# RMS norm and matmul on one core: another order of rows in the eight-tile transfers

## The chip, the cores and the metric

The kernel runs on one core of a Trainium2 chip. The metric is the device time in microseconds. A profile of one execution comes beside it, whose span is a little shorter than the time. The engines of a core are TensorE (PE; its weight loads are PEld), VectorE (DVE), ScalarE (ACT), GpSimd (POOL) and SyncE (SP), which here only issues transfers. Sixteen DMA engines carry these transfers between DRAM and SBUF, the on-chip memory of 128 partitions.

## What is computed

Each row of x is divided by its root mean square, scaled by gamma and multiplied by a weight matrix:

```python
def reference(x, gamma, weight, eps):          # x: 16 x 1024 x 512 float32
    rms = np.sqrt(np.mean(x ** 2, axis=-1, keepdims=True) + eps)
    x_norm = x / rms * gamma                   # gamma: 512
    return np.matmul(x_norm, weight).astype(np.float32)   # weight: 512 x 768
```

There are 16 x 1024 = 16,384 rows. 33.6 MB of x come in, 50.3 MB of results go out, and rows are independent of each other, so that it doesn't matter which row lies in which partition as long as its result goes back to the same row.

## The kernel before

The rows are cut into 128 tiles of 128 rows, one row in each partition. A tile is cast to bf16 (`cast`, L93), transposed by TensorE (`transpose_word`, L120), copied out of PSUM by VectorE (`evac`, L127) and multiplied with the weights in four steps of 128 (`matmul`, L155). Gamma has been folded into the weights at the start. Meanwhile ScalarE squares and sums the rows (`square`, L97), and takes the root (`root`, L101); VectorE takes the reciprocal (L103). The result of a tile is scaled by it on its way from PSUM to the output tile: even tiles by ScalarE (L137), odd tiles by VectorE (L139). Casts are GpSimd's, but for the opening. Most of this goes in pairs of tiles: a loop over 64 pairs from L266 issues, for each pair, the cast of a pair three ahead, the squares of the next, and the matmuls of this one with transposes of a pair two ahead between them. The order within each engine is written out by hand (`tc.manual_schedule`), so the program's order is the order of issue.

Rows come and go in groups of G = 8 tiles, NG = 16 groups in all. A group has one input tile `xt` of 128 partitions x 8 x 512 float32 (five such buffers, L65) and one output tile `ot` of 128 x 8 x 768 float32 (three, L72). Which row of DRAM lies in which partition is set by one function, `rows` (L59). For the first group (i < G) it serves small pieces, of one and two tiles. For the others partition p holds the eight consecutive rows 8p to 8p + 7 of the group's 1,024, one for each of its eight tiles. In DRAM these are one stretch of 8 x 512 x 4 bytes = 16 KB of x, or 8 x 768 x 4 bytes = 24 KB of out, and the partitions follow each other without a gap.

All large transfers are issued by SyncE, in one queue. `load` (L82) brings a group, or a part of it where `stretches` says so (group 1 comes as two halves of four tiles). `store` (L152) sends a group once its last tile is scaled; group 14 goes as two halves, and group 15 as pieces of 2, 2, 2, 1 and 1 tiles. `load_until(2 * j + AHEAD)` with AHEAD = 28 (L267) issues a load some 28 tiles ahead of the pair that TensorE works on. As both kinds stand in one queue, a load issued behind a store goes out after the store's own wait for the outputs.

Of the kernel before, what the change touches and what calls it, by code (L numbers as in the profile page):

```python
# [18 lines left out]
def kernel(  # L19
# [9 lines left out]
    P = 128  # L29
# [8 lines left out]
    G = 8  # L38
# [4 lines left out]

    def stretches(parts):
        first, size, i = {}, {}, 0
        for g in range(NG):
            for n in parts.get(g, [G]):
                for t in range(i, i + n):  # L50
                    first[t], size[t] = i, n
                i += n
        return first, size

    opening = [1, 2, 1, 2, 2]
    x_first, x_size = stretches({0: opening, 1: [4, 4]})
    o_first, o_size = stretches({0: opening, NG - 2: [4, 4], NG - 1: [2, 2, 2, 1, 1]})

    def rows(ap, i, n):  # L59
        if i < G:  # L60
            return ap[i * P:(i + n) * P, :].rearrange("(p t) d -> p t d", t=n)
        return ap.rearrange("(g p t) d -> g p t d", p=P, t=G)[i // G, :, i % G:i % G + n, :]

    singles = ctx.enter_context(tc.tile_pool(name="singles", bufs=1))
    xin = ctx.enter_context(tc.tile_pool(name="xin", bufs=5))  # L65
# [13 lines left out]
    def load(i):  # L79
        if i // G not in x_tiles:  # L80
            x_tiles[i // G] = xin.tile([P, G, D], F32, name="xt")
        nc.sync.dma_start(out=held(x_tiles, i, x_size[i]), in_=rows(x, i, x_size[i]))  # L82
# [58 lines left out]
    def accumulator():  # L141
        return opsum.tile([P, 2, WIDE], F32, name="ops").rearrange("p a b -> p (a b)")
# [6 lines left out]
    def store(i):  # L149
        first, n = o_first[i], o_size[i]  # L150
        if i == first + n - 1:
            nc.sync.dma_start(out=rows(out, first, n), in_=held(o_tiles, first, n))  # L152
# [32 lines left out]
    with tc.manual_schedule():  # L185
# [80 lines left out]
        for j in range(2, NP):  # L266
# [15 lines left out]
            for i, engine in ((2 * j, nc.scalar), (2 * j + 1, nc.vector)):  # L282
                a = accumulator()
# [4 lines left out]
        for i in (NT - 2, NT - 1):  # L288
            for lo, hi, engine in ((0, WIDE, nc.scalar), (WIDE, O, nc.vector)):
                a = accumulator()  # L290
# [39 lines left out]
```

## Time and profile before

| What | Value |
|---|---|
| time, median of 3 runs | 211.11 us (210.84 to 211.83) |
| span of the profiled execution | 209.0 us |
| TensorE busy | 198.7 us (95%) |
| ScalarE busy | 158.3 us (76%) |
| VectorE busy | 111.6 us (53%) |
| GpSimd busy | 66.4 us (32%) |
| DRAM read, written | 35.13 MB, 50.33 MB |
| mean rate of the DMA engines | 410 GB/s |
| stores of eight tiles, 13 | 3,072 KB each, 20.5 us from issue to landing (median) |
| loads of eight tiles, 14 | 2,048 KB each, 24.9 us from issue to landing (median) |

The shares are of the span and overlap, since the engines work side by side. Landing is when the transfer's last byte is reported; the time from issue to landing holds the wait behind transfers issued earlier. In the lines that follow, a name such as `xb L93` is a tile and the line of the program that made it, and `A <- B` in a table of waits says that A stood idle until B was done.

### The profile page before, as it was taken

The numbers are of one execution on the slowest core, as the hardware profiler recorded it, in microseconds if no ns is written. First come the engines' busy times: TensorE is split into PE (matmuls) and PEld (weight loads), VectorE is DVE, ScalarE is ACT, GpSimd is POOL, SyncE is SP. The second block draws the span as 40 slices with busy tenths as digits, with TensorE's granted clock in tenths as the row PEclk, the third lists the DMA queues.
The fourth block names the chain that finished last, engine by engine and source line by source line (L and its number), as shares of the span: only waits on it lengthen the run. The fifth ranks groups of instructions, "written<-read, shape, count | busy, mean of one in ns | idle before, by whom it ended". The sixth has DMA issues, their size and how long they took to land.

```text
span 209.0 us, 3555 instructions
## 1 busy us (share of the span) xinstructions
PE 198.7 (95%) x1268; PEld 137.5 (66%) x1293; DVE 111.6 (53%) x204; ACT 158.3 (76%) x388; POOL 66.4 (32%) x71
## 2 busy tenths in 40 slices
PE   7899999999999999999999999999999999999960
PEld 3466776667666776677666766676666766776630
DVE  2566565466456545644654565466456545645630
ACT  4599678778877877887787778778777877887830
POOL 1165443233323323332332333233223323310000
PEclk9999999999999999999999999999999999999997
DMA  6999999999999999999999999999999999998983
GB/s 223 413 426 444 396 404 422 423 448 411 433 426 417 455 415 442 408 439 415 423 448 415 445 408 448 430 415 444 408 444 423 434 437 426 409 423 357 412 347 142
DMA packets 7206, 85.69 MB, mean 410 GB/s; under 512 B 1042, under 2 KB 1044, under 8 KB 3220
## 3 DMA queue, kind: packets, MB, share of 16 engines
q1 hardware_dynamic: 6912, 85.46, 97.0%
q8 instruction: 10, 0.16, 0.3%
q10 hardware_dynamic: 276, 0.00, 0.1%
q14 instruction: 8, 0.07, 0.1%
HBM read 35.13 MB, written 50.33 MB: 409 GB/s over the span
## 4 chain that ended last, share of the span: by engine, by line
PE 93%; DVE 2%; issue 1%; ACT 1%
PE ops L155 78%; PE tp L120 13%; PE ops L210 1%; DVE ot L139 1%; DVE xT L127 1%; ACT ot L137 0%; ACT jk L97 0%; DVE xb L93 0%; DVE w_bf L139 0%; PE tp L224 0%; ACT rms L101 0%; DVE warm L201 0%; DVE rstd L103 0%; DVE eps_sb L203 0%
## 5 line engine op out<-in xcount | busy, mean ns | idle before, releaser
L155 PE MATMUL ops<-w_bf,xT 128*128 128x512 bf16 (+1 forms) x999 | 192.5, 324 | 1.9 <-DVE w_bf L139 0.6
L155 PEld LDWEIGHTS <-xT 128*128 128x128 bf16 x1024 | 100.2, 98 | 57.0 <-issue 1.0
L93 POOL CAST xb<-xt 128x1024 bf16<-128x1024 f32 (+1 forms) x65 | 65.7, 1016 | 118.5 <-PE tp L120 108.1
L127 DVE COPY xT<-tp 128x1024 bf16<-128x1024 bf16 (+1 forms) x67 | 44.5, 667 | 80.8 <-PE tp L120 80.8
L137 ACT ACTIVATE ot<-ops,rstd 128x768 f32<-128x768 f32 (+1 forms) x65 | 58.1, 894 | 37.7 <-PE ops L155 36.9
L97 ACT ACTIVATE jk<-xt 128x512 bf16<-128x512 f32 x128 | 78.8, 619 | 1.2 <-DMA xt<-in_x_dram 1.2
L120 PE MATMUL tp<-ident_f,xb 128*128 128x128 f32 x256 | 69.0, 274 | 0.3 <-DVE xb L93 0.2
L139 DVE TENSOR_SCALAR ot<-ops,rstd 128x768 f32<-128x768 f32 (+1 forms) x65 | 64.5, 992 | 2.9 <-PE ops L155 2.8
L120 PEld LDWEIGHTS tp<-ident_f,xb 128*128 128x128 f32 x256 | 35.9, 141 | 3.8 <-issue 0.8
L97 ACT ACTIVATION_READ_ACCUMULATOR jk<-xt 128x1 f32 x128 | 24.4, 190 | 0.0
L101 ACT ACTIVATE rms<-ssq,eps_sb 128x2 f32<-128x2 f32 (+1 forms) x64 | 18.9, 295 | 2.0
L103 DVE RECIPROCAL rstd<-rms 128x2 f32<-128x2 f32 (+1 forms) x64 | 9.9, 155 | 3.2 <-ACT rms L101 3.1
L210 PE MATMUL ops<-warm 128*128 128x512 bf16 x11 | 4.5, 555 | 1.2 <-DVE eps_sb L203 1.2
L210 PEld LDWEIGHTS <-warm 128*128 128x128 bf16 x11 | 1.4, 134 | 2.6 <-issue 1.4
L137 ACT ACTIVATE w_bf<-w_f,g_sb 128x768 bf16<-128x768 f32 x2 | 1.9, 936 | 1.4 <-DMA w_f<-in_weight_dram 0.7
L192 ACT ACT_TABLE_LOAD x1 | 1.3, 1283 | 1.8 <-issue 1.8
L93 DVE CAST xb<-xt 128x512 bf16<-128x512 f32 x2 | 1.1, 530 | 2.5 <-DMA xt<-in_x_dram 2.5
L139 DVE TENSOR_SCALAR w_bf<-w_f,g_sb 128x512 bf16<-128x512 f32 (+2 forms) x3 | 1.4, 480 | 0.5 <-DMA w_f<-in_weight_dram 0.5
L224 PEld LDWEIGHTS tp<-ident_f,g_row 2*128 2x128 f32 x2 | 0.3, 200 | 0.8 <-issue 0.8
L201 DVE MEMSET warm<- 128x256 uint32 x1 | 0.3, 272 | 0.9 <-PEq L311 0.9
L224 PE MATMUL tp<-ident_f,g_row 2*128 2x2 f32 x2 | 0.4, 264 | 0.0
masks.py:199 POOL TENSOR_SCALAR_AFFINE_SELECT ident_f<-ident_f 128x128 f32<-128x128 f32 x1 | 0.3, 294 | 0.1
(7 smaller groups left out, 0.8 us busy)
## 6 DMA issues: line engine op xcount, KB each, us to landing
out_dram<-ot SPq DMA_DIRECT2D x13, 3072.0 KB, 20.5
xt<-in_x_dram SPq DMA_DIRECT2D x14, 2048.0 KB, 24.9
out_dram<-ot SPq DMA_DIRECT2D x6, 768.0 KB, 7.0
out_dram<-ot SPq DMA_DIRECT2D x2, 1536.0 KB, 9.0
xt<-in_x_dram SPq DMA_DIRECT2D x2, 1024.0 KB, 11.1
xt<-in_x_dram SPq DMA_DIRECT2D x3, 512.0 KB, 5.7
w_f<-in_weight_dram SPq DMA_DIRECT2D x2, 768.0 KB, 6.0
out_dram<-ot SPq DMA_DIRECT2D x4, 384.0 KB, 17.9
```

Of the source, the lines that this page charges most:

```text
L93: engine.tensor_copy(out=xb_tiles[i // 2][:, i % 2:i % 2 + n, :], in_=held(x_tiles, i, n))
L97: nc.scalar.activation(out=jk, in_=held(x_tiles, i)[:, 0, :], func=AF.Square, accum_out=ssq)
L101: nc.scalar.activation(out=rms[:, :n], in_=ssq[:, :n], func=AF.Sqrt, scale=1.0 / D, bias=eps_sb)
L103: nc.vector.reciprocal(out=rstd[:, :n], in_=rms[:, :n])
L120: nc.tensor.transpose(out=tp_tiles[j][:, t, h, :], in_=words[:, lo:lo + P], identity=ident_f)
L127: nc.vector.tensor_copy(out=dst[:, t:t + n, :], in_=src[:, t:t + n, :])
L137: nc.scalar.mul(out=dst, in_=src, mul=r)
L139: nc.vector.tensor_single_scalar(out=dst, in_=src, scalar=r, op=mybir.AluOpType.mult)
L155: nc.tensor.matmul(out=acc[:, lo:hi], lhsT=xT_tiles[i // 2][:, i % 2, k // 2, :, k % 2], rhs=w_bf[:, k, lo:hi], start=(k == 0), stop=(k == ...
L192: nc.scalar.preload_act_table(AF.Sqrt)
L210: nc.tensor.matmul(out=spare[:, :WIDE], lhsT=warm[:, :P], rhs=warm, start=True, stop=True)
L224: nc.tensor.transpose(out=gp[:, c, :], in_=g_row[:, :, c], identity=ident_f[:2, :2])
```

## The change

One line in `rows` differs. A group's 1,024 rows were split as (p t), with p the partition. Now they are split as (b a t), with a = 16 and b = 8, and the partition is 8a + b. A partition still holds eight consecutive rows, so the stretches keep their length, but stretch number 16b + a in DRAM now goes to partition 8a + b, where stretch number p went to partition p. The same function serves loads and stores, so that each row's result returns to its place.

```diff
     def rows(ap, i, n):
         if i < G:
             return ap[i * P:(i + n) * P, :].rearrange("(p t) d -> p t d", t=n)
-        return ap.rearrange("(g p t) d -> g p t d", p=P, t=G)[i // G, :, i % G:i % G + n, :]
+        return ap.rearrange("(g b a t) d -> g a b t d", a=16, b=P // 16, t=G)[i // G, :, :, i % G:i % G + n, :]
```

The idea is this. If each of the 16 DMA engines carries eight neighbouring partitions, as the change assumes, then engine a carries the eight values of b for its a. Before, that was a block of eight stretches of its own, far from those of the other engines. After, the 16 engines in step work on the 16 stretches of one b, which lie side by side in DRAM, and then all move on to the next 16. On the DRAM side the pattern now has two dimensions where it had one, 16 by 8 in place of 128.

## The prediction

> **What bounds the kernel now.** I read the share of each engine and the DMA line first, then the chain of waits, the table of who waited for whom, the issues of the DMA queue in order of time, and last a table of 10 us windows. On the page:
>
> ```profile
> span 209.0 us, 3555 instructions
> ...
> PE   7899999999999999999999999999999999999960
> ...
> DMA  6999999999999999999999999999999999998983
> ...
> q1 hardware_dynamic: 6912, 85.46, 97.0%
> ...
> PE 93%; DVE 2%; issue 1%; ACT 1%
> ```
>
> Two rows are full in nearly every slice: TensorE, and the mean of the 16 DMA engines. The last line is the chain that ended last: 93% of it is TensorE, so today TensorE sets the end. But the DMA engines have nothing to spare. Queue 1 moved 85.46 MB in 97.0% of 16 engines' 209.0 us, which is 0.970 x 16 x 209.0 = 3,244 us of engine time, or 85.46 MB / 3,244 us = 26.3 GB/s for one busy engine. Who waits for whom:
>
> ```profile
> POOL xb L93 <- PE tp L120: 108.1, 53, 4.5
> DVE xT L127 <- PE tp L120: 80.8, 63, 1.4
> ACT ot L137 <- PE ops L155: 36.9, 62, 1.3
> POOL xb L93 <- DMA xt<-in_x_dram: 9.8, 4, 3.9
> ```
>
> The columns are us in total, how often, and the longest. The engines wait for TensorE. Waits of the casts for loaded rows are 9.8 us in 4 pieces, and no line says that an output tile waited for an earlier store. The rhythm is in the DMA queue's issues (start, us):
>
> ```profile
> 58.47 0.33 SPq L152 DMA_DIRECT2D out_dram<-ot  x1
> 58.90 0.88 SPq L82 DMA_DIRECT2D xt<-in_x_dram  x1
> 70.62 0.33 SPq L152 DMA_DIRECT2D out_dram<-ot  x1
> 71.04 0.81 SPq L82 DMA_DIRECT2D xt<-in_x_dram  x1
> ```
>
> One store of eight tiles and one load of eight tiles go out every 70.62 - 58.47 = 12.15 us, TensorE's time for eight tiles. They carry 3,072 + 2,048 KB = 5.243 MB, so the pace asks for 5.243 MB / 12.15 us = 431.5 GB/s. The windows say what is delivered (the last two columns are the DMA share and GB/s):
>
> ```profile
> 100.00:110.00 10.00, 9.95 (x67) 6.98 (x66) 5.95 (x11) 7.89 (x21) 3.57 (x4) 1.00 1.01 433
> ...
> 200.00:210.00 10.00, 2.07 (x14) 1.13 (x12) 1.50 (x3) 1.37 (x2) 0.00 (x0) 0.84 0.55 220
> ```
>
> Demand and supply meet to within a per cent. A store issued at 46.3 us lands after 20.2 us and one issued at 143.5 us after 21.1 us: the queue in front of the engines neither empties nor grows much. So TensorE is the bound by name and the DMA engines are a second bound just underneath; whatever makes a transfer slower comes out in the time.
>
> [...]
>
> **The change part by part.** In the built program the instructions are the same in number and order on every engine; only the shapes of the transfers differ. A store's DRAM side was 128x6144 and is 16x8x6144. This holds for every transfer of groups 1 to 15 (G = 8 and i >= G in `rows`), the four-, two- and one-tile pieces among them; the opening eight tiles and the weights keep their form.
>
> 1. What stays, at cost nothing: bytes, number of transfers, the length of a stretch (16 KB of x, 24 KB of out, since t and d are still neighbours in DRAM), partitions and TensorE's work. The queue's issue of a transfer, 0.33 to 0.96 us, may grow with one dimension more; SyncE waits 168.6 us of the span for VectorE's outputs, which hides a doubling of some 45 issues.
>
> 2. The order in DRAM. Stretch p = 8a + b moves from place p to place 16b + a. Consecutive stretches of a partition run are now 256 KB (x) or 384 KB (out) apart. [...] I put the cost at zero. The gain is bounded by what is lost now[...] and hidden under TensorE except after its end. TensorE ends at about 202 us; the last store (384 KB, issued at 202.7) lands 5.4 us later. A 256 KB load of the opening landed 2.9 us after its issue, so 384 KB with the engines free would take about 2.9 + 128 KB / 431.5 GB/s = 3.2 us. At most 2.2 us is to be had.
>
> 3. Which engine touches which partition. This is the part that decides. [...]
>
> What is stretched: 15 groups x 12.15 us = 182.3 us of the DMA engines' time. The DMA engines are full now, and buffers can't pay for a lower rate: an output buffer (three of eight tiles) is wanted again two groups, 24.3 us, after its store, which lands in 20.5 us; 3.8 us of slack, once. Behind a late landing stand the scalings of ScalarE and VectorE (L137, L139), behind them TensorE for an accumulator. Behind a late load stand GpSimd's cast and ScalarE's squares, then the transposes. So the time is 211.1 + 182.3 x (f - 1).
>
> f is not in the trace. [...] I take 1.65[...]: 211.1 + 182.3 x 0.65 = 330 us. The ends kept for the range are f = 1.1 (229 us) and f = 2.0 (393 us).
>
> **The rivals.** (a) Sharing hurts in one direction only, or softly. Loads are 15 x 2.097 = 31.5 MB, at 431.5 GB/s 73 us; doubled alone they give 284 us. Soft sharing, f from 1.05 to 1.4, gives 220 to 284. [...] (b) No change: the engines are dealt out as before[...]. TensorE's 12.15 us stays the pace: 211 us. For it: TensorE has 93% of the chain, and 26.3 GB/s may be an engine's own limit. [...] (c) Faster: neighbouring stretches save waits in DRAM and the engines end more evenly. It can take only from the 2.2 us of the drain; half of it gives 210.0 us. [...]
>
> **How the numbers follow.** Forecast, sharing in both directions with f from 1.4 to 2.0: 0.60. Rival (a): 0.25. Rival (b): 0.08. Rival (c): 0.07. Slower by over 0.5% is 0.60 + 0.25 = 0.85. The range from 228 to 394 leaves out (b) and (c), 0.15, and about 0.05 of the softest sharing and of anything worse than in step.
>
> **What would show it.** If right: the DMA row stays near full while the rate falls from 410 towards 85.69 MB / 328 us = 261 GB/s; store and load landings grow from 20.5 and 24.9 us by the same factor or more; waits for xt and for the stores of ot appear among the engines' own; TensorE's busy share falls to about 198.7 / 328 = 61% with the same number of instructions and the same means for scalings and casts. Step 2 is wrong if the rate falls although one engine's partitions stay as before, or if only the order of rows without the shape of 16 does it. Step 3 is wrong if the rate stays at 410 GB/s and the store interval at 12.15 us; the prediction then falls as a whole. If only loads are long, rival (a) holds.

## The result, and the profile after

The changed kernel takes 255.69 us (median of 6 runs, 252.79 to 256.92) where the kernel before takes 211.16 us (median of 6). That is 44.5 us more. Runs within 1.5% of the fastest count as fast, and the ratio of fast runs alone is 1.203, with a 95% interval from 1.194 to 1.212. The row of rates before the change, and then the page of the changed kernel:

```profile
GB/s 223 413 426 444 396 404 422 423 448 411 433 426 417 455 415 442 408 439 415 423 448 415 445 408 448 430 415 444 408 444 423 434 437 426 409 423 357 412 347 142
```

```profile
span 251.0 us, 3555 instructions
...
DMA  7999999999999999999999999999999999999940
GB/s 260 388 225 225 230 221 323 301 281 248 338 341 300 411 326 428 367 418 394 413 375 401 422 422 409 418 419 418 410 394 437 416 394 380 394 320 299 306 165 22
...
q1 hardware_dynamic: 6912, 85.46, 95.5%
...
DMA 53%; PE 32%; DVE 3%; ACT 2%; issue 1%; POOL 0%; ACTq 0%; SPq 0%
...
out_dram<-ot SPq DMA_DIRECT2D x13, 3072.0 KB, 29.6
xt<-in_x_dram SPq DMA_DIRECT2D x14, 2048.0 KB, 34.8
```

The DMA engines are as full as before, yet move less. The row GB/s, one number for each of 40 slices (of 6.3 us in the changed kernel), tells where. After the opening it falls to 221 to 230 for four slices, half of the 431.5 GB/s that TensorE asks for. Then it climbs, is at 394 to 437 in most slices of the middle, and drops again in the last five. The loss is thus not spread over the run. More than half of the chain is now transfers. The table of who waited for whom has lines that were not there or were small:

```profile
POOL xb L94 <- DMA xt<-in_x_dram: 50.4, 14, 8.7
ACT ot L138 <- DMA out_dram<-ot: 42.1, 10, 8.2
...
DVE ot L140 <- DMA out_dram<-ot: 18.6, 9, 5.9
PE ops L156 <- ACT ot L138: 17.0, 9, 5.6
```

GpSimd's casts wait for loaded rows (50.4 us, before 9.8), and both scaling engines wait for an output buffer whose store has not landed; behind them TensorE waits for an accumulator. The store issues give the delay group by group (start, us):

```profile
68.30 0.59 SPq L153 DMA_DIRECT2D out_dram<-ot  x1
...
88.14 0.59 SPq L153 DMA_DIRECT2D out_dram<-ot  x1
...
102.19 0.59 SPq L153 DMA_DIRECT2D out_dram<-ot  x1
...
156.81 0.59 SPq L153 DMA_DIRECT2D out_dram<-ot  x1
...
168.96 0.59 SPq L153 DMA_DIRECT2D out_dram<-ot  x1
```

The first two are 19.84 us apart; the last two are at TensorE's old 12.15 us. Before the change, the store of group 5, third in these lines, went out here:

```profile
82.76 0.33 SPq L152 DMA_DIRECT2D out_dram<-ot  x1
```

Against the same stores before, group 5 is 102.19 - 82.76 = 19.4 us late, group 11 is 181.27 - 155.64 = 25.6 us late, the last store is 232.7 - 202.7 = 30.0 us late, and the end is 42.0 us late. So 19.4 us go in the first five groups, 6.2 in the next six, 4.4 in the rest, and 12.0 after the last store's issue, which lands 17.3 us later where it took 5.4. Three questions follow. Is it the shape of 16 or the order in DRAM? Do both directions suffer? Why does the rate recover, and then fall again?

### The profile page after: what moved, and what is told of

Same layout as the page of the kernel before. It is cut to its first block, busy times and chain, and to the rows that moved or that the text cites. A ratio compares the mean times of both kernels' runs of the same rounds, so it can differ in the third digit from the quotient of the medians.

```text
span 251.0 us, 3555 instructions
## 1 busy us (share of the span) xinstructions
PE 204.3 (81%) x1268; PEld 138.8 (55%) x1293; DVE 114.9 (46%) x204; ACT 155.8 (62%) x388; POOL 66.1 (26%) x71
## 3 DMA queue, kind: packets, MB, share of 16 engines
q1 hardware_dynamic: 6912, 85.46, 95.5%
## 4 chain that ended last, share of the span: by engine, by line
DMA 53%; PE 32%; DVE 3%; ACT 2%; issue 1%; POOL 0%; ACTq 0%; SPq 0%
DMA out_dram<-ot 53%; PE ops L156 26%; PE tp L121 4%; DVE ot L140 2%; ACT ot L138 2%; PE ops L211 2%; POOL xb L94 0%; DVE xT L128 0%; ACT jk L98 0%; DVE w_bf L140 0%; PE tp L225 0%; ACT rms L102 0%; DVE warm L202 0%; ACTq L138 0%; SPq L153 0%
## 5 line engine op out<-in xcount | busy, mean ns | idle before, releaser
L156 PE MATMUL ops<-w_bf,xT 128*128 128x512 bf16 (+1 forms) x999 | 197.5, 328 | 18.9 <-ACT ot L138 17.0
L156 PEld LDWEIGHTS <-xT 128*128 128x128 bf16 x1024 | 101.3, 99 | 58.7 <-issue 3.1
L94 POOL CAST xb<-xt 128x1024 bf16<-128x1024 f32 (+1 forms) x65 | 65.4, 1015 | 147.6 <-PE tp L121 88.7
L121 PE MATMUL tp<-ident_f,xb 128*128 128x128 f32 x256 | 69.9, 277 | 6.5 <-POOL xb L94 6.4
## 6 DMA issues: line engine op xcount, KB each, us to landing
out_dram<-ot SPq DMA_DIRECT2D x13, 3072.0 KB, 29.6
xt<-in_x_dram SPq DMA_DIRECT2D x14, 2048.0 KB, 34.8
out_dram<-ot SPq DMA_DIRECT2D x2, 1536.0 KB, 20.5
```

The costliest lines, as they stand in the source:

```text
L94: engine.tensor_copy(out=xb_tiles[i // 2][:, i % 2:i % 2 + n, :], in_=held(x_tiles, i, n))
L121: nc.tensor.transpose(out=tp_tiles[j][:, t, h, :], in_=words[:, lo:lo + P], identity=ident_f)
L156: nc.tensor.matmul(out=acc[:, lo:hi], lhsT=xT_tiles[i // 2][:, i % 2, k // 2, :, k % 2], rhs=w_bf[:, k, lo:hi], start=(k == 0), stop=(k == ...
```

## The experiments

The expectations weigh two theories. By the DRAM-order theory the wider steps of a partition run in DRAM slow the transfers. "Ports theory" is their name for the sharing that the forecast assumed: with the shape 16x8 DMA engines slow each other while they are in step. f is the factor by which the transfers of groups 1 to 15 then take longer, and a lag is the distance between two engines, in us or in packets (a packet is what is moved for one partition). The traces show the slowing: between 20 and 40 us a load's packet of 16 KB takes 1.25 us in the changed kernel, where it took 0.61 before (medians). They don't show which engine carries which partitions, nor which engines slow each other and through what; the pairs of the expectations are an assumption.

### The order in DRAM without the slowest dimension of 16

```diff
-        return ap.rearrange("(g b a t) d -> g a b t d", a=16, b=P // 16, t=G)[...]
+        return ap.rearrange("(g b a t) d -> g a b t d", a=32, b=P // 32, t=G)[...]
```

> Neighbouring stretches in DRAM for the 16 engines as in the changed kernel (partition 4a + b holds stretch 32b + a), but the slowest dimension is 32[...]. Ports theory [...]: back to 211 us, within 2 us, TensorE's 12.15 us a group and over 425 GB/s in the steady part. DRAM-order theory (the wide steps in DRAM slow the reads and writes): about as slow as the changed kernel, 245 to 260 us.

211.08 us (median of 14), ratio to the kernel before 0.9994, interval 0.998 to 1.0008. Its page:

```profile
GB/s 225 410 430 435 402 400 420 410 451 412 437 438 413 443 410 437 419 430 433 413 438 427 441 423 432 429 418 440 416 443 419 432 446 421 390 437 355 398 350 147
...
q1 hardware_dynamic: 6912, 85.46, 96.9%
...
PE 93%; DVE 2%; ACT 1%; issue 1%
```

The steps of a partition run in DRAM are even wider here (512 KB of x, 768 KB of out), and the pattern has two dimensions as well. Neither costs anything, and neighbouring stretches bring nothing that shows either.

### The slowest dimension of 16 without the order

```diff
-        return ap.rearrange("(g b a t) d -> g a b t d", a=16, b=P // 16, t=G)[...]
+        if i // G == NG - 1:
+            return ap.rearrange("(g p t) d -> g p t d", p=P, t=G)[i // G, :, i % G:i % G + n, :]
+        pairs = ap[G * P:(NG - 1) * G * P, :].rearrange("(q a s b t) d -> q s a b t d", a=16, s=2, b=P // 16, t=G)
+        return pairs[(i // G - 1) // 2, (i // G - 1) % 2, :, :, i % G:i % G + n, :]
```

> The shape of the changed kernel (slowest dimension 16) in groups 1 to 14, [...] blocks of two groups alternate, so that the dimensions stay apart. Group 15 is as before. Ports theory: 240 to 262 us, with some 225 GB/s in the first groups. DRAM-order theory: 211 us.

255.51 us (median of 4, 253.09 to 260.27), ratio 1.2004 (1.1964 to 1.2044): the whole loss. Its page, of the execution of 260.27 us, shows the same course, the halved start, the climb and the late drop:

```profile
GB/s 214 395 228 233 213 224 337 287 293 228 382 306 328 393 351 394 357 418 413 404 404 415 428 416 407 415 423 420 431 352 417 361 316 255 293 278 311 317 178 23
```

Eight neighbouring partitions have one block of eight neighbouring stretches here, as before the change. Whether eight neighbouring partitions are one engine's, which the section on the change assumes, no trace shows, for this order or for that of before. With the run above this still settles the first question: with 16 as the slowest dimension on the DRAM side some 44 us are lost in two different orders of rows, and with 32 nothing.

### One direction at a time

```diff
-    def rows(ap, i, n):
+    def rows(ap, i, n, new):
...
+        if not new:
+            return ap.rearrange("(g p t) d -> g p t d", p=P, t=G)[i // G, :, i % G:i % G + n, :]
...
```

`new` is true for loads in one run and for stores in the other.

> Only the loads have the changed form; stores have the old one, so the rows of the result stand in another order within their group. Ports theory: [...] the changed kernel's packets of loads took longest, so most of its 44 us stay: 228 to 245 us, stores unhurt. If only the DRAM side of stores mattered: 211 us.

> Only the stores have the changed form; loads have the old one, so the rows of the result stand in another order within their group. Ports theory [...]: 225 to 260 us. Sharing that hurts loads alone: 211 to 214 us.

Loads alone: 257.86 us (249.90 to 267.57, 4 runs). Stores alone: 242.26 us (234.55 to 247.34, 4 runs). Both directions suffer, and the two don't add up: by their fastest runs they cost 39 and 24 us, where both together cost 42. The rows of rate, loads alone first, are of the slowest execution of each, 267.57 and 247.34 us:

```profile
GB/s 260 360 231 224 217 212 402 222 299 240 420 285 334 365 256 417 282 351 383 292 418 330 356 392 340 429 360 417 388 391 402 329 337 370 99 370 367 362 364 22
```

```profile
GB/s 257 419 435 422 372 422 422 351 254 306 407 270 351 383 326 388 350 386 391 394 402 404 419 422 420 422 422 398 418 390 379 344 195 264 246 287 346 328 124 28
```

With loads alone the dips go on into the last quarter. With stores alone the first seven slices are untouched, since the early transfers are loads, and the dips come with the large stores; the late drop is there too, whereas loads alone run at 362 to 370 near the end, but for one slice. The late drop thus goes with stores in the form 16x8 in these executions.

### The engines alone

All computing is left out. Sixteen loads, then sixteen stores go through the queue, once in each form:

```python
for g in range(NG):
    xt = xin.tile([P, G, D], F32, name="xt")
    nc.sync.dma_start(out=xt, in_=rows(x, g))
for g in range(NG):
    nc.sync.dma_start(out=rows(out, g), in_=ot)
```

> All computing is left out: 16 loads of eight tiles, then 16 stores of eight tiles of zeros, one after the other in the queue, in the old form (one dimension of 128). Measures the engines alone: 33.6 + 50.3 MB at about 430 GB/s, 195 us and a few us for start and end, with the same rate in loads and in stores.

> The same with the changed form (16x8): all computing left out, 16 loads, then 16 stores. If [...] nothing moves them apart, they stay in step: 215 GB/s throughout, 156 us of loads and 234 us of stores, about 393 us. If the arbitration itself, or chance, moves them apart: the rate starts at 215 and climbs to 350 or more within the loads, 230 to 300 us. If stores don't share: 156 + 117 = 275 us, with 430 GB/s in the second part.

200.72 and 289.29 us (one run each, as for all runs without computing). Windows of 10 us; the last column is GB/s. The old form (one dimension of 128), in its loads and in its stores:

```profile
40.00:50.00 10.00, 0.00 (x0) 0.00 (x0) 1.00 1.02 436
140.00:150.00 10.00, 0.00 (x0) 0.00 (x0) 1.00 1.00 433
```

The form 16x8:

```profile
20.00:30.00 10.00, 0.00 (x0) 0.00 (x0) 1.00 1.00 224
130.00:140.00 10.00, 0.00 (x0) 0.00 (x0) 1.00 1.00 224
160.00:170.00 10.00, 0.00 (x0) 0.00 (x0) 1.00 0.98 251
190.00:200.00 10.00, 0.00 (x0) 0.00 (x0) 1.00 0.99 364
230.00:240.00 10.00, 0.00 (x0) 0.00 (x0) 1.00 1.01 435
```

Loads stay at half the rate from first to last, about 150 us without a sign of recovery. Stores begin nearly as low and are above 430 some 60 us later, and stay there nearly to the end: with the same shape and no change in the program.

The trace also keeps the times of the 16 landings of each transfer, which I take as one for each engine. The 16 landings of every load in the form 16x8 fall within 0.8 us: the engines are in step, and stay so. Those of its stores, one store after the other, are spread over 1.5, 2.9, 4.4, 6.5, 8.7 and 10.1 us, and then steadily over 10.5 to 10.8 us. So stores do move the engines apart. The packets tell more. A load's packet of 16 KB takes 0.96 to 1.24 us (5% to 95%, window of 130 to 140 us), where the old form has 0.61. A store's packet of 24 KB takes 0.91 to 2.09 us (160 to 170 us), where the old form has 0.91. The packets of loads are slowed nearly alike; of stores some are hardly slowed and others more than doubled. Unequal packets would move engines apart, but why stores are unequal isn't shown.

Then stores ahead of loads (the two loops exchanged):

> The pure stream in the form 16x8, with the 16 stores ahead of the 16 loads (all computing left out). If stores move a pair apart by themselves: the rate climbs from 215 to 430 GB/s within some 60 us of stores. [...] In all 60 x 0.5 + 117 = 147 us and 33.6 MB / 287 = 117 us: 255 to 275 us. If it was time and not stores that moved them: loads at 430, some 225 us.

274.71 us:

```profile
20.00:30.00 10.00, 0.00 (x0) 0.00 (x0) 1.00 0.96 248
60.00:70.00 10.00, 0.00 (x0) 0.00 (x0) 1.00 0.99 371
110.00:120.00 10.00, 0.00 (x0) 0.00 (x0) 1.00 1.01 433
160.00:170.00 10.00, 0.00 (x0) 0.00 (x0) 1.00 1.01 239
240.00:250.00 10.00, 0.00 (x0) 0.00 (x0) 1.00 1.02 328
```

Stores recover again within some 70 us, so it is stores and not the time since the start. Then loads fall back to 239, and climb slowly to 328: loads that begin out of step don't stay as they are. The steady 287 that I expected isn't there; the total came out right by chance of its parts.

### Setting the lag of a pair

By the forecast's assumption only the distance between two engines matters. So small added transfers, one on 12 engines and one on 4, were to hold some engines back against the others. The pure stream with both has 528 packets under 512 B, 16 more than the 512 (16 for each transfer) of 32 large transfers alone, which fits 12 and 4; which engines they are isn't shown. The first tries put added loads ahead of the large ones: seven packets an engine in the changed kernel, and as its control the same loads spread evenly; four packets in the pure stream and in the changed kernel. The edit for four packets:

```diff
+        nc.sync.dma_start(out=spare_x[40:88, :], in_=xs[0:48, :].rearrange("(k m) c -> m k c", k=4))
+        nc.sync.dma_start(out=spare_x[88:104, :], in_=xs[48:64, :].rearrange("(k m) c -> m k c", k=4))
```

> The changed kernel with two more loads of rows that nothing uses, ahead of group 1: one on 12 engines and one on 4, seven packets of 16 KB for each engine. [...] each pair [...] starts 7 x 0.61 = 4.3 us apart, more than the 3.7 us of half a store. Ports theory with the step of the pairs as the cause: no dip to 225 GB/s at the start beyond the added loads themselves, and 214 to 230 us in all (1.8 MB more to move, 4 to 9 us). If the step doesn't matter: as the run with even added loads, within a few us.

> The changed kernel with the same 1.8 MB of rows that nothing uses, loaded on all 16 engines alike (seven packets each), so that the pairs stay in step. Ports theory: as the changed kernel and up to 9 us on top, 252 to 266 us, with the dip to some 225 GB/s in the first groups.

> The pure stream in the form 16x8 (all computing left out, 16 loads, then 16 stores), with two small loads ahead, one on 12 engines and one on 4, four packets of 16 KB for each engine[...]. [...] If the step of a pair is all that costs: loads at about 430 GB/s from the first and not at 226, 78 us for them; [...] 203 to 215 us in all, where the same stream without the offset took 289. If the form costs in itself: 285 to 295 us.

> The changed kernel with the added loads of four packets for each engine on 12 and on 4 engines, ahead of group 1 (1.0 MB that nothing uses): half a load apart, where the seven packets of the earlier try were one short of a whole transfer of eight and so left the loads of groups 1 to 3 almost in step. If the step is all that costs: no dip to 225 GB/s in the first 35 us, and only the stores' part of the sharing until they move apart: 214 to 235 us. If lag isn't the cause: 250 to 262 us.

Offset of seven: 247.68 us (ratio 1.170, 1.165 to 1.174); even added loads: 260.35 us (1.232, 1.226 to 1.239); four in the kernel: 248.79 us (238.04 to 254.74); four in the pure stream: 271.78 us. An offset helps, by 12.7 us against the even loads, but by far less than I expected, and loads in the pure stream went at only 242 to 270 GB/s between 20 and 130 us; two of the windows:

```profile
60.00:70.00 10.00, 0.00 (x0) 0.00 (x0) 1.00 0.98 261
100.00:110.00 10.00, 0.00 (x0) 0.00 (x0) 1.00 1.00 251
```

The issues of that run show a fault in the design (start and duration, us):

```profile
0.73 0.99 SPq L50 DMA_DIRECT2D spare_x<-in_x_dram  x1
1.78 0.69 SPq L51 DMA_DIRECT2D spare_x<-in_x_dram  x1
2.52 99.12 SPq L54 DMA_DIRECT2D xt<-in_x_dram  x16
```

The first large load was issued 2.52 - 0.73 = 1.8 us after the first added one. The engines that were meant to run ahead had nothing to do until then, so by my estimate, of a lead of 4 x 0.61 = 2.4 us (packets of the old form) some 0.6 us was left. I had not looked at what the queue holds when the offset is made. The second set therefore fills the queue first, with two loads in the old form, and offsets with small stores, which read SBUF and don't write it:

```diff
+        for g in range(2):   # two loads of eight tiles in the old form
+            ...
+        nc.sync.dma_start(out=behind(0, 12), in_=zeros[40:88, :C])    # 12 engines, 4 packets each
+        nc.sync.dma_start(out=behind(48, 4), in_=zeros[88:104, :C])   # 4 engines, 4 packets each
```

> Computing left out: 2 loads of eight tiles in the old form, which fill the queue; then small stores on 12 and on 4 engines, four packets of 8 KB for each engine; then 14 loads and 15 stores of eight tiles in the form 16x8. The last group's output is not computed. Each pair starts two load packets (of 16 KB) apart. [...] 286 GB/s, steady through all 14 loads. About 255 us in all. If the form costs in itself: 226 GB/s as without an offset, some 290 us.

> The same with 16 KB for each of the four packets: four load packets apart. Eight packet times, 4.9 us a load, 429 GB/s, steady; about 212 us in all if the stores then part quickly. If the form costs in itself: 226 GB/s.

> The same with the small stores given twice: eight load packets apart, a whole transfer, which brings each pair into step again. 215 to 230 GB/s in the loads, about 290 us in all. If any lag at all helped, it would be over 400 GB/s.

> As with four packets apart, but without the small store on 4 engines[...]. If the slowest pair sets the pace (a buffer is free only when all 16 engines have landed it, and there are five): some 330 GB/s for the first few loads, then 226 to 240. If pairs were independent: 330 GB/s throughout the loads.

273.86, 210.22, 257.40 and 276.05 us. The window of 60 to 70 us, among the loads, for intended lags of 2, 4 and 8 packets, and for 4 with the small store on 12 engines alone:

```profile
60.00:70.00 10.00, 0.00 (x0) 0.00 (x0) 1.00 1.03 228
```

```profile
60.00:70.00 10.00, 0.00 (x0) 0.00 (x0) 1.00 0.99 377
```

```profile
60.00:70.00 10.00, 0.00 (x0) 0.00 (x0) 1.00 1.03 233
```

```profile
60.00:70.00 10.00, 0.00 (x0) 0.00 (x0) 1.00 0.99 220
```

The landings say what was really set. Loads of the run of 4 land 5.5 us after each other, in three bunches (the first 4 landings, the next 8, the last 4) some 2.5 us apart: nearly half a transfer, as planned. In the run of 8, loads land 9.2 us after each other, and of the two distances one is 8.4 us, nearly a whole transfer, but the other only 5.3 us. In the run of 2 the distances are about 2.0 and 1.0 us of 9.5, one to two packets. A lag in time is a smaller part of a transfer where loads land 9.5 us after each other and not 5.5.

So the same loads in the same shape go at 377 GB/s (429 was expected) when the bunches are nearly half a transfer apart, and in step at 224, half of the old 436. In the run of 8 the bunches are further apart than in the run of 4 (8.4 and 5.3 us against 2.5), and the rate is 233: a later start alone isn't what helps. That the place within the transfer does is my reading of these runs. With 377 and 224 GB/s in one form, the cost is in how the engines meet and not in the form itself. No run tests the 286 expected at a lag of two packets; the 228 were measured at distances of 2.0 and 1.0 us, one to two packets.

With the small store on 12 engines alone, which was to part half of the pairs (4.5 us of 9.4), the rate is 220, that of none apart. I had expected the parted engines to be quick and then wait for the others. They don't wait: the DMA share is 0.99, and the packets of loads between 60 and 70 us take 1.02 to 1.25 us (5% to 95%), hardly one near 0.61. The parted engines are slow as well. Pairs that have nothing to do with other pairs, as the forecast assumed them, don't explain that; what couples the engines is open.

## Why the prediction was right and wrong

**The bound, right.** The DMA engines were the second bound just underneath (97.0% of their time taken by queue 1 before, 95.5% after), and what made transfers slower came out in the time.

**Step 1, right but for TensorE.** Instructions and bytes are the same, and the means of scalings and casts too (ACT 888 ns, before 894; DVE 995, before 992; casts 1,015, before 1,016). TensorE's work, put at no cost, took 204.3 us where it had taken 198.7; its granted clock was 0.83 in the window of 30 to 40 us and 0.71 in that of 70 to 80 us, in which it had to wait, against 1.00 before. How much of these 5.6 us the waits hide is not shown. The issue of a store grew from 0.33 to 0.59 us, of a load up to 2.4 us, hidden.

**Step 2, right.** The order in DRAM is worth 0 +- 0.2% (0.998 to 1.0008 with 32x4). The steps of 512 and 768 KB there cost nothing that shows. For the smaller steps of the change, 256 and 384 KB, no cost was my estimate; blocks_16x8, which is without them, loses as much (ratio 1.2004). The 2.2 us of the drain were not to be had by this order.

**Step 3, right in kind.** 16x8 loses all of it in two orders of rows, 32x4 nothing, and the same shape goes at 220 or at 377 GB/s by how far the engines are apart. The start, with 216 GB/s between 20 and 40 us, is 431.5 / 216 = 2.0 times slower: in step, as the upper end had it, and the packets there take 1.25 us for 0.61. What the engines share, and which partitions each of them carries, was assumed and isn't shown; only the slowing in step is, by the times. That pairs are independent of each other is not borne out (220 GB/s with the store on 12 engines alone, above).

**The term that failed: f, held to be one number for all 182.3 us.** I forecast f = 1.65, or 119 us more; 44.5 us were measured, f = 1 + 44.5 / 182.3 = 1.24. The forecast loss was more than twice the measured one. The 1.65 was my estimate, put between engines whose distance wanders evenly and engines that keep the distance with which they began. Neither case let the lag move one way and settle. Loads alone in the queue do keep step, for about 150 us at some 224 GB/s. But stores move the engines apart within some 60 us, and end near f = 1 (above 430 GB/s). The kernel mixes both, and its own landings show the course: the 16 landings of a transfer span 0.7 us at 16 to 21 us, 2.6 us at 65 us, 8.0 us at 104 us and 10.3 us at 192 us (before the change 0.3 us at the start and some 3.7 us from 92 us on). So it begins at f = 2, is near 1.05 in the window of 150 to 160 us (409 GB/s), and pays most of its loss in the first five groups and in the end.

At the end, with the loads gone, stores drop to about 300 GB/s. A distance that suits loads and stores in turn need not suit stores alone; that is argued from the drop that the three rows with stores in the form 16x8 have (changed kernel, old blocks, stores alone) and the one with loads alone has not, and it was not isolated. A rival is the smaller pieces in which the last two groups go: the streams of loads, then stores, have no such pieces, and their stores stay near 430 GB/s until the last 20 us. Why the two directions don't add up is open too. With loads alone in the form 16x8 the landings also spread, from 1.5 us at 16 us to 15 us at 110 us, and the time stays well below the 284 us of loads that keep half the rate to the end.

**The rivals.** (a), one direction: both cost alone. (b) and (c): 32x4 stays at the old time (211.08 us); 16x8 is neither unchanged nor faster.

**What was to be seen.** Landings grew by 29.6 / 20.5 = 1.44 and 34.8 / 24.9 = 1.40, more than the time's 1.20, as said; the new waits are the ones named; TensorE is busy for 81%, not 61%, and the rate is 341 GB/s, not 261, both by the same wrong f.

## What to carry to other kernels

When the partitions of an SBUF tile are composed of two dimensions in DRAM, look at the slowest of them: 16 kept the 16 engines full (95.5% of their time) and still cost 20% here, while 32 cost nothing (ratio 0.9994). If the mean rate of full DMA engines falls, read the row of GB/s slice by slice before taking a mean: here 216 GB/s in one stretch and 409 in another came from how the engines met, and the order in memory had no part in it that showed. Before an experiment that shifts transfers in time, look at what the queue holds at that moment, and afterwards read from the landings what shift was really there.

## What the hardware showed that I had not expected

Loads in the form 16x8, alone in the queue, kept the engines in step and at half the rate for about 150 us. Stores in the same form moved them apart, from 1.5 to 10.7 us between the first and the last landing, and came to above 430 GB/s within some 60 us. Loads whose engines landed in three bunches, nearly half a transfer apart (2.5 of 5.5 us), went at 377 GB/s; with the small store on 12 engines alone (4.5 of 9.4 us) they went at 220, no faster than with all in step.
